# Even mixer: queries' projection first, the convolution's mean ahead of the attention, three sets of head buffers, and reciprocal roots on VectorE

## The chip, the cores and the metric

The kernel runs on one core of one Trainium2 chip. TensorE (PE) multiplies matrices into eight banks of accumulators (PSUM), VectorE (DVE), ScalarE (ACT) and GpSimd (POOL) work on tiles of 128 partitions, and the DMA queues, above all that of SyncE (SP), bring weights from memory. The metric is the device time of one execution in microseconds (us), lower is better; the time given is the median of three runs.

## The reference

Two trunk layers work on 512 latent tokens and 256 context tokens of width 1024. Each layer is a modulated half-step feed-forward block (width 2816), a token mixer, and another such block. Layer 0 has the even mixer, layer 1 the odd one. The change is in the even mixer and in one helper that all norms over the model width use. What the even mixer computes, cut to its core:

```python
def rms_norm(x, g):   # x * rsqrt(mean(x*x) + EPS) * g
def layer_norm(x, g, b):   # (x - mu) * rsqrt(var + EPS) * g + b
def conv_module(u, prm):
    a, g = split(u + glu_b); y = a * sigmoid(g)
    y = depthwise_conv(y, width 31) + dw_b            # 512 channels
    return silu(layer_norm(y, ln_g, ln_b))
def mla_kv(pp, prm, rope):                            # 8 heads
    kvu = rms_norm(pp[..., :256], kv_norm) @ w_ukv    # -> k_nope (64) and v (64) of each head
    k = concat(rms_norm(k_nope), rope(rms_norm(pp[..., 256:288])))
def mla_q(pp, prm, rope):
    q = rms_norm(pp[..., 288:672], q_norm) @ w_uq     # 64 + 32 of each head, both normed, 32 rotated
def even_mixer(hl, hc, prm, ...):
    att = attention(q, k, v)      # latent queries: keys of context and latent; context queries: context keys
    return concat([att, conv_module(pl[..., 672:])]) @ w_out
```

## The kernel before

Products in full fp32 precision are formed as three products of rounded parts: each operand is split into a high part `hi` (a cast, L210) and a low part `lo` (a subtraction, L211), and `hi*hi + lo*hi + hi*lo` is summed in a PSUM bank (L190). PSUM is used as two pairs of banks called `pa`, one pair called `pb`, and two single banks `p`; the helper `pd()` goes round pa, pa, pb. The feed-forward blocks are long rows of such products. A scheduler orders what is not pinned on each engine by its own estimates; instructions passed through `pin` keep their order.

The even mixer before its attention: the input products give the low-rank rows (`natA`, 256 wide, for keys and values; `natB`, 384 wide, for queries). `lora_t` (L869, L871) transposes them on TensorE and splits them. Then come, for each of the six token tiles, the keys' and values' products with `w_ukv` (`up_tile`; ScalarE copies the key part out at L888, the value part at L889 and squares the keys at L891; VectorE sums the squares at L894, takes the root and scales the keys by it, L196); the transposes of `natB`; the rotation of the keys' last 32 columns; and the queries' six tiles with `w_uq`, evacuated at L951, L952 and L954, whose roots, scaling and rotation VectorE does. Head 0's keys and queries are then transposed in four quarters of three tiles each (`quarter`: transposes L923, the high part on ScalarE L926, the low part on VectorE L929).

The attention is a pipeline of 48 items, eight heads of six query tiles, pinned (`flow`). An item has scores (S, L1003), exponentials (L633), a reciprocal of the row sum (L624), a scaling on GpSimd (L625), transposes (L617) and the product with the values (L664); VectorE's row maximum of the scores is L630. Query tiles 0 to 3 see 768 keys, tiles 4 and 5 (context) see 256. In items 1 to 4 of a head the next head's four quarters are formed. The layer norm of the convolution rides in the same pipeline: a list of steps (`conv_ln`), one taken at the end of each item from item `LN0` on. Before, these steps are: the mean over channels in two pieces (L765: ones times the four channel tiles, in one PSUM bank; L770: four subtractions that read the bank), the squares on ScalarE with sums on GpSimd (`sq`, L778), and the reciprocal root, whose steps are `rb_steps`: sums over partitions (L269), `rstd` (L244 to L249: mean plus epsilon on VectorE, Sqrt on ScalarE at L245 with a table load, reciprocal and one Newton step on VectorE), a diagonal matrix (L274), a product that spreads it over partitions (L279) and a copy to the tile `rb` (L282). `rb_steps` stands at nine places of the program, the others in the norms of the feed-forward blocks and mixers.

Another background work is the modulation rows (`mod_dve`): VectorE multiplies rows of the modulation weights by the tile `cb` (128x2048), which holds silu of the conditioning vectors. `cb` is loaded from `in_cB` (L328), put through Silu (L329), and kept.

Of the kernel before, what the change touches and what calls it, by code (L numbers as in the profile page):

```python
# [19 lines left out]
NT = NL + NC  # L20
# [14 lines left out]
LN0 = 8  # L35
# [55 lines left out]
class Kern:  # L91
# [143 lines left out]
    def rstd(self, ss, n, inv_n, mul=None, pin=lambda i: i):  # L235
# [23 lines left out]
    def rb_steps(self, inv_n, nt, pin, buf, t0=0):  # L259
# [11 lines left out]
        def f1():  # L271
            r = self.rstd(c["ps"][:, :k], k, inv_n, None, pin)
# [484 lines left out]
    def conv_ln(self):  # L757
# [4 lines left out]
        def mean(a, b, o):  # L762
            mu = self.p1()[:, 0:b - a]
            for c in range(4):
                pin(nc.tensor.matmul(mu, self.ones, cv[c][:, o:o + b - a], start=c == 0, stop=c == 3))  # L765

            def f():
                for c in range(4):
                    y = cv[c][:, o:o + b - a]
                    pin(nc.vector.scalar_tensor_tensor(y, mu, -1.0 / 512, y, op0=ALU.mult, op1=ALU.add))  # L770
            return f
# [42 lines left out]
    def even_mixer(self):  # L814
# [44 lines left out]

        cq6 = self.rows("B", NT, 6)  # L860
# [21 lines left out]
        Kp = [a.rearrange("p (t h e) -> p t h e", t=2, e=96) for a in Ka]
        for t in range(6):
            i = t % 2
            p = self.pd()
            self.up_tile(p, ckh, ckl, t, wk, 0, 512)
            self.up_tile(p[:, 512:1024], ckh, ckl, t, wk, 512, 512)
            (nc.scalar.copy if EVB[1] else nc.vector.tensor_copy)(K[t][:, :, 0:64], h8(p[:, 0:512]))  # L888
            nc.scalar.copy(V[t], p[:, 512:1024])  # L889
            sq = self.t768()  # L890
            nc.scalar.activation(sq[:, 0:512], p[:, 0:512], AF.Square)  # L891
            if i == 0:
                sK = self.stat(16)
            nc.vector.tensor_reduce(sK[:, i * 8:i * 8 + 8], h8(sq[:, 0:512]), axis=AX.X, op=ALU.add)  # L894
            if i:
                rK = self.rstd(sK, 16, 1.0 / 64)
                kn = Kp[t // 2][:, :, :, 0:64]
                self.tt(kn, kn, rK.rearrange("p (t h) -> p t h", t=2).unsqueeze(3).broadcast_to((128, 2, 8, 64)), ALU.mult, QN_E(nc))
        lora_t(natB, cqh, cql, 3, "qg")
# [719 lines left out]
```

## Time and profile before

| what | value |
|---|---|
| median of three runs | 2865.4 us (2865.26 to 2869.09) |
| profiled execution | 2866.91 us, its span 2865.0 us |
| PE busy | 2792.8 us, 97% of the span |
| DVE busy | 1588.1 us, 55% |
| ACT busy | 858.3 us, 30% |
| POOL busy | 317.0 us, 11% |
| mean granted TensorE clock | 0.99 |
| even mixer, from the keys' and queries' projections to the fourth head | 752.5 to 889.0 us of the span |
| first scores of the attention | 812.53 us |

The busy shares are means over the whole span; the last line names the stretch in which the change works. "Granted clock" is the share of full speed that the chip allowed TensorE in a stretch. A row of a timeline gives start, duration, engine, line, operation, tile written and tiles read, and in square brackets how long the engine had been idle before it and what ended that idle time.

### The profile page before, as it was taken

Reading aid. Unit: us, or ns where it says so; the run is one execution under the profiler, and the core shown is the slowest. Engines: PE = TensorE matmul, PEld = TensorE weight load, DVE = VectorE, ACT = ScalarE, POOL = GpSimd, SP = SyncE. Lnnn points to the kernel's source line nnn. Section 1 sums busy time; section 2 is a strip of 40 time slices with the busy share of each in tenths; the row PEclk is TensorE's granted clock in tenths of the full one; section 3 lists DMA queues with packets and bytes.
Section 4 is the critical chain, followed back from the end, with each engine's and each line's share of the span. In section 5 each row is a group of like instructions: output and inputs, shape, how many; then the busy total and the mean of one; then the engine's idle time right before and its main releaser. Section 6 shows DMA issues by size and latency. Waiting matters only on the chain.

```text
span 2865.0 us, 41335 instructions
## 1 busy us (share of the span) xinstructions
PE 2792.8 (97%) x17180; PEld 2429.3 (85%) x17180; DVE 1588.1 (55%) x2618; ACT 858.3 (30%) x1284; POOL 317.0 (11%) x357
## 2 busy tenths in 40 slices
PE   7999999999978999999999999999999999999999
PEld 5888888887767788888888888888887878898998
DVE  2674675678565576747535432333347689644443
ACT  3221212242456422122122221221224267322222
POOL 1000000030022320000002100000021156300000
PEclk9999999999989999999999999999999999999999
DMA  6343343442200224426411121212133200322232
GB/s 234 126 149 109 116 156 104 133 138 75 72 30 20 63 95 130 151 89 208 160 66 60 60 67 59 66 54 69 61 101 114 60 12 31 96 92 93 90 102 89
DMA packets 80042, 272.22 MB, mean 95 GB/s; under 512 B 9456, under 2 KB 11248, under 8 KB 79728
## 3 DMA queue, kind: packets, MB, share of 16 engines
q1 hardware_dynamic: 72048, 252.11, 27.4%
q10 hardware_dynamic: 6144, 12.23, 1.4%
q0 software_dynamic: 1664, 5.24, 0.5%
q8 instruction: 136, 2.23, 0.3%
q14 instruction: 50, 0.41, 0.0%
HBM read 258.10 MB, written 7.34 MB: 93 GB/s over the span
## 4 chain that ended last, share of the span: by engine, by line
PE 64%; DVE 2%; ACT 1%; DMA 1%; issue 1%; POOL 0%; ACTq 0%; DVEq 0%; POOLq 0%
PE pa L190 39%; PE pb L190 19%; PE p L664 2%; PE pb L617 2%; DMA m<-in_modt 1%; PE pa L1229 1%; PE pa L1003 1%; ACT t L619 0%; DVE sm L630 0%; DVE m L339 0%; PE p L279 0%; PE pa L1255 0%; DVE wl L211 0%; PE p L1217 0%; ACT t L803 0%
## 5 line engine op out<-in xcount | busy, mean ns | idle before, releaser
L210 ACT CAST wh<-r 128x1024 fp32r<-128x1024 f32 (+3 forms) x334 | 341.7, 1023 | 1494.1 <-PE pa L190 778.4
L190 PE MATMUL pa<-B,wh 128*128 128x258 f32 (+2 forms) x1952 | 481.4, 328 | 2.7 <-ACT B L386 2.7
L190 PE MATMUL pa<-C,wh 128*128 128x258 f32 (+2 forms) x1952 | 481.7, 328 | 0.3 <-DVE C L387 0.3
L190 PE MATMUL pa<-B,wl 128*128 128x258 f32 (+2 forms) x1952 | 478.3, 326 | 0.0
L211 DVE TENSOR_TENSOR wl<-r,wh 128x1024 fp32r<-128x1024 f32 (+3 forms) x334 | 400.5, 1199 | 43.6 <-ACT wh L210 37.2
L190 PEld LDWEIGHTS pa<-B,wh 128*128 128x128 f32 x1952 | 303.6, 190 | 37.5 <-ACT B L386 2.7
L190 PEld LDWEIGHTS pa<-C,wh 128*128 128x128 f32 x1952 | 303.4, 190 | 35.0 <-issue 0.7
L190 PEld LDWEIGHTS pa<-B,wl 128*128 128x128 f32 x1952 | 303.6, 190 | 34.6
L190 PE MATMUL pa<-E,wh 128*128 128x512 f32 (+1 forms) x937 | 258.9, 345 | 1.8 <-POOL E L215 1.2
L190 PE MATMUL pb<-B,wh 128*128 128x512 f32 (+1 forms) x992 | 244.3, 327 | 0.0
L190 PE MATMUL pb<-C,wh 128*128 128x512 f32 (+1 forms) x992 | 243.4, 327 | 0.0
L190 PE MATMUL pb<-B,wl 128*128 128x512 f32 (+1 forms) x992 | 242.7, 326 | 0.0
L475 DVE COPY sm<-pa 128x2 f32<-128x2 f32 x115 | 18.2, 158 | 403.2 <-PE pa L190 403.2
L190 PE MATMUL pa<-D,wh 128*128 128x512 f32 (+1 forms) x800 | 207.0, 337 | 0.7 <-ACT D L227 0.6
L190 PE MATMUL pa<-D,wl 128*128 128x256 f32 (+1 forms) x752 | 200.1, 339 | 0.0
L339 DVE SCALAR_TENSOR_TENSOR m<-m,cb 128x1024 f32<-128x1024 f32 x128 | 157.1, 1230 | 28.9 <-DMA m<-in_modt 28.3
L190 PEld LDWEIGHTS pa<-E,wh 128*128 128x128 f32 x937 | 150.2, 188 | 24.8 <-POOL E L215 1.6
L190 PEld LDWEIGHTS pb<-B,wl 128*128 128x128 f32 x992 | 153.9, 190 | 17.9 <-issue 0.5
L190 PEld LDWEIGHTS pb<-B,wh 128*128 128x128 f32 x992 | 153.7, 189 | 17.8 <-issue 1.5
L190 PEld LDWEIGHTS pb<-C,wh 128*128 128x128 f32 x992 | 153.4, 189 | 17.1 <-issue 0.2
L190 PEld LDWEIGHTS pa<-D,wh 128*128 128x128 f32 x800 | 125.4, 188 | 19.9 <-ACT D L227 0.9
L199 DVE SCALAR_TENSOR_TENSOR A<-pa,hg,A 128x256 f32<-128x256 f32 (+1 forms) x96 | 55.3, 613 | 144.8 <-PE pa L190 144.8
(328 smaller groups left out, 4197.7 us busy)
## 6 DMA issues: line engine op xcount, KB each, us to landing
m<-in_modt SPq DMA_DIRECT2D x128, 512.0 KB, 4.2
r<-in_win0a SPq DMA_DIRECT2D x44, 512.0 KB, 3.5
r<-in_win0b SPq DMA_DIRECT2D x44, 512.0 KB, 3.5
r<-in_win1a SPq DMA_DIRECT2D x44, 512.0 KB, 3.4
r<-in_win1b SPq DMA_DIRECT2D x44, 512.0 KB, 3.4
r<-in_wodd SPq DMA_DIRECT2D x18, 512.0 KB, 3.8
r<-in_wout0a SPq DMA_DIRECT2D x20, 448.0 KB, 3.9
r<-in_wout1a SPq DMA_DIRECT2D x20, 448.0 KB, 3.3
```

The costliest lines, as they stand in the source:

```text
L190: self.nc.tensor.matmul(out, l.bitcast(F32R), r.bitcast(F32R), start=st, stop=sp)
L199: self.nc.vector.scalar_tensor_tensor(o, a, s, b, op0=op0, op1=op1)
L210: pin(self.nc.scalar.copy(hi, r))
L211: pin(self.nc.vector.tensor_tensor(lo, r, hi.bitcast(F32), op=ALU.subtract))
L339: nc.vector.scalar_tensor_tensor(o, u, 1.0, self.cb[:, v * 1024:(v + 1) * 1024], op0=ALU.mult, op1=ALU.mult, accum_out=self.mod[L][:, f, v ...
L475: nc.vector.tensor_copy(w2[:, o:o + 2], p[:, so:so + 2])
L617: pin(nc.tensor.transpose(pt[:, ks], P[:, ks], self.col("ident")))
L664: self.pin(self.nc.tensor.matmul(self.po[i * 64:(i + 1) * 64, col:col + 128], v, self.PTs[i][:, kt * 128:(kt + 1) * 128], start=(kt == 0), ...
L1003: self.pin(nc.tensor.matmul(s[:, o:o + b - a], q[:, ts].bitcast(F32R), k[:, a:b].bitcast(F32R), start=j == 0, stop=j == 2))
L1229: self.pin(nc.tensor.matmul(s[:, a:b], q.bitcast(F32R), k[:, a:b].bitcast(F32R), start=j == 0, stop=j == 1))
```

## The change

1. Both `lora_t` stand together, and the queries' products come before the keys' and values'.
2. The weights `w_ukv` are split earlier, before the transposes. Their parts go to the two halves of the tile `cb`, to the area `E3` and to a tile of the `m` pool; therefore `cb` is loaded and put through Silu once more afterwards.
3. The convolution's mean is formed ahead of the attention: eight matmuls into one `pa` pair, one copy by ScalarE with the factor -1/512 into `rb`. In the pipeline four steps `centre` add `rb` to the channel tiles on VectorE, from SBUF alone.
4. Head 0's quarters all come after the keys, queries first, in three rotating pairs (`pd()`).
5. The three sets of head buffers are B0/B1, B3/C3 and E2/E3 in this order.
6. `LN0` goes from 8 to 4, and empty steps (`no`) stand between the squares and between the root's steps.
7. In `rb_steps`, at all nine places, the reciprocal root is taken on VectorE: the value's bits, taken as an integer, are shifted right by one and subtracted from 0x5f3759df, and three Newton steps follow. ScalarE has no Sqrt there any more. The other roots (keys, queries, low-rank rows) keep Sqrt.

```diff
-LN0 = 8
+LN0 = 4
@@ rstd(..., bits=False)
-        pin(nc.scalar.activation(s, v, AF.Sqrt))
-        pin(nc.vector.reciprocal(r, s))
-        pin(nc.vector.scalar_tensor_tensor(t, r, -0.5, v, op0=ALU.mult, op1=ALU.mult))
...
+        if bits:
+            pin(nc.vector.tensor_scalar(s.bitcast(I32), v.bitcast(I32), 1, None, op0=ALU.logical_shift_right))
+            pin(nc.vector.tensor_scalar(r.bitcast(I32), s.bitcast(I32), -1.0, float(0x5f3759df), op0=ALU.mult, op1=ALU.add))
+        else:
+            pin(nc.scalar.activation(s, v, AF.Sqrt))
+            pin(nc.vector.reciprocal(r, s))
+        for _ in range(3 if bits else 1):
+            pin(nc.vector.scalar_tensor_tensor(t, r, -0.5, v, op0=ALU.mult, op1=ALU.mult))
+            pin(nc.vector.tensor_tensor(t, t, r, op=ALU.mult))
+            pin(nc.vector.scalar_tensor_tensor(r, t, 1.5, r, op0=ALU.add, op1=ALU.mult))
@@ conv_ln
+        def centre(c):
+            for a, b, o in LNREG:
+                y = cv[c][:, o:o + b - a]
+                pin(nc.vector.tensor_tensor(y, y, self.rb[:, a:b], op=ALU.add))
-        st = [lambda r=r: mean(*r) for r in LNREG]
-        st += [lambda c=c: sq(c) for c in range(4)]
-        st += [lambda: mm(0), lambda: None, lambda: mm(2), lambda: mm(4)]
+        no = lambda: None
+        st = [lambda c=c: (lambda: centre(c)) for c in range(4)]
+        st += [f for c in range(4) for f in (lambda c=c: sq(c), no)]
+        st += [no, lambda: mm(0), no, no, lambda: mm(2), no, lambda: mm(4), no]
@@ even mixer
+        X = self.cbt()
+        self.cb = None
+        E3 = self.area("E3")
+        wk = []
+        for k, (hi, lo) in enumerate(((X[:, 0:1024], X[:, 1024:2048]), (E3[:, 0:1024], self.mt()))):
+            r = self.raw(self.I["wukv"][k], 1024)
+            self.split(hi, lo, r)
+            wk.append((hi, lo))
...
         lora_t(natA, ckh, ckl, 2, "kvg")
+        lora_t(natB, cqh, cql, 3, "qg")
...  (the loop over the keys' and values' tiles now stands behind that of the queries)
+        bufs = [self.rows(t, NT, 4) for t in (["B0", "B1"], ["B3", "C3"], ["E2", "E3"])]
...
+        mu = self.pd()
+        for a, b, o in LNREG:
+            for c in range(4):
+                nc.tensor.matmul(mu[:, a:b], self.ones, self.cv[c][:, o:o + b - a], start=c == 0, stop=c == 3)
+        nc.scalar.activation(self.rb, mu[:, 0:NT], AF.Copy, scale=-1.0 / 512)
+        for j in (2, 3, 0, 1):
+            quarter(0, j, lambda i: i)
```

The lines of the changed kernel are shifted: 7 more in most of the program (L190 is L191, L244 is L246, L274 is L281, L624 is L631), and L923, L926, L929, L1003 are now L972, L975, L978, L1019.

On TensorE, directly ahead of the attention, the rows before are the last products of a query tile (B parts of the low-rank queries against weights), then half of head 0's transposes, here the two quarters of the queries (E and C hold queries):

```order
L190 MATMUL pa_6437<-wh_6254,B_710_5989 128x256
L190 MATMUL pa_6437<-wl_6255,B_709_5988 128x256
L923 MATMUL pb_6545<-small,E_764_6225 96x128 x2
L923 MATMUL pb_6545<-small,E_765_6226 96x128
L923 MATMUL pb_6551<-small,E_765_6226 96x128
L923 MATMUL pb_6551<-small,C_766_6227 96x128 x2
L1003 MATMUL pa_6557<-B_762_6223,C_763_6224 128x512
```

and in the changed kernel the last products are those of a key and value tile, and the mean (L986) and all four quarters (queries in E and C, keys in A) stand between them and the first scores:

```order
L191 MATMUL pb_6451<-E_709_6006,C_717_6020 128x512
L191 MATMUL pb_6451<-m_6007,B_716_6019 128x512
L986 MATMUL pa_6548<-D_610_4934,ones 128x512 x2
L986 MATMUL pa_6548<-D_611_4935,ones 128x512 x2
L986 MATMUL pa_6548<-D_610_4934,ones 128x256 x2
L986 MATMUL pa_6548<-D_611_4935,ones 128x256 x2
L972 MATMUL pa_6558<-small,E_732_6094 96x128 x2
L972 MATMUL pa_6558<-small,E_733_6095 96x128
L972 MATMUL pa_6570<-small,A_723_6066 96x128 x2
L972 MATMUL pa_6576<-small,A_725_6068 96x128 x2
L1019 MATMUL pa_6584<-B_806_6542,B_807_6543 128x512
```

The mean has moved out of the pipeline to this place, and two quarters more stand in it.

On ScalarE at the same place, the rows before are the queries' last evacuation (L954 squares, L245 the root), two casts of weights of the output product (L210) and the two high parts of head 0's queries:

```order
L954 ACTIVATE t_6458<-pa_6437 128x768
L926 ACTIVATE C_763_6224<-pb_6545,ones 96x384
L210 CAST wh_8215<-r_8213 128x1024
L245 ACTIVATE st_6463<-st_6462 128x32
L210 CAST wh_8279<-r_8277 128x1024
L926 ACTIVATE C_763_6224<-pb_6551,ones 96x384
L633 ACT_TABLE_LOAD
L633 ACTIVATE t_6566,sm_6567<-pa_6557,sm_6564 128x768
```

and in the changed kernel they are the keys' last evacuation and root, the second Silu of `cb` with its table load, the mean's copy (L987) and four high parts:

```order
L949 COPY A_725_6068<-pb_6451 128x8x64
L950 COPY C_778_6335<-pb_6451 128x512
L952 ACTIVATE t_6466<-pb_6451 128x512
L251 ACTIVATE st_6470<-st_6469 128x16
L336 ACT_TABLE_LOAD
L336 ACTIVATE cb_8698<-cb_8698 128x2048
L987 ACTIVATE rb<-pa_6548 128x768
L975 ACTIVATE B_807_6543<-pa_6558,ones 96x384
L975 ACTIVATE B_806_6542<-pa_6576,gcomb 96x384
L640 ACT_TABLE_LOAD
L640 ACTIVATE t_6593,sm_6594<-pa_6584,sm_6591 128x768
```

The reload of `cb` has come in between the keys' root and the high parts that the first scores read.

On VectorE, the convolution's root in the pipeline before (between a low part of a quarter and the next item's reciprocal):

```order
L929 SCALAR_TENSOR_TENSOR B_762_6223<-p_6960,gcomb,B_762_6223 96x384
L244 TENSOR_SCALAR sm_7001<-p_6965 128x6
L246 RECIPROCAL sm_7003<-sm_7002 128x6
L247 SCALAR_TENSOR_TENSOR sm_7004<-sm_7003,sm_7001 128x6
L248 TENSOR_TENSOR sm_7004<-sm_7004,sm_7003 128x6
L249 SCALAR_TENSOR_TENSOR sm_7003<-sm_7004,sm_7003 128x6
L274 TENSOR_TENSOR m_7011<-small,sm_7003 128x768
L624 RECIPROCAL sm_7023<-sm_6945 128x1
```

and in the changed kernel:

```order
L637 TENSOR_REDUCE sm_7092<-pa_7068 128x1
L246 TENSOR_SCALAR sm_7104<-p_7082 128x6
L248 TENSOR_SCALAR sm_7105<-sm_7104 128x6
L249 TENSOR_SCALAR sm_7106<-sm_7105 128x6
L254 SCALAR_TENSOR_TENSOR sm_7107<-sm_7106,sm_7104 128x6
L255 TENSOR_TENSOR sm_7107<-sm_7107,sm_7106 128x6
L256 SCALAR_TENSOR_TENSOR sm_7106<-sm_7107,sm_7106 128x6
...
L281 TENSOR_TENSOR m_7120<-small,sm_7106 128x768
L631 RECIPROCAL sm_7131<-sm_7054 128x1
```

The Sqrt between the first two rows is gone, and the three Newton rows stand there three times; the root has moved behind the quarters, to the last item of head 2.

## Rows read from the trace of the kernel before

**Rows 1.** Busy time of each engine by stage, then the granted clock.
```profile
core 0: us, PE busy (x) PEld busy (x) DVE busy (x) ACT busy (x) POOL busy (x), PEclk, DMA share, GB/s
752.50:776.80 24.30, 21.23 (x107) 16.83 (x102) 13.44 (x26) 16.15 (x31) 0.00 (x0) 1.00 0.09 27
776.80:801.20 24.40, 22.13 (x116) 18.61 (x116) 19.88 (x61) 10.59 (x22) 0.00 (x0) 0.93 0.07 23
801.20:812.50 11.30, 1.27 (x7) 0.55 (x5) 10.67 (x22) 5.12 (x9) 0.00 (x0) 0.63 0.38 128
812.50:823.90 11.40, 10.98 (x56) 9.14 (x54) 7.18 (x13) 8.94 (x17) 2.71 (x3) 0.77 0.03 12
823.90:844.60 20.70, 18.74 (x136) 14.30 (x135) 11.76 (x28) 11.38 (x24) 4.55 (x6) 1.00 0.00 1
844.60:874.60 30.00, 22.22 (x144) 17.42 (x142) 10.53 (x26) 16.28 (x33) 10.81 (x10) 0.77 0.06 18
874.60:889.00 14.40, 13.93 (x128) 11.91 (x127) 11.56 (x26) 10.61 (x23) 4.03 (x6) 1.00 0.11 38
```

**Rows 2.** Timeline of TensorE, a wait between two stages of products.
```profile
776.82 1.20 PE L190 MATMUL pa<-wh,B 128*128 128x512 f32 x2 [0.97 <-DVE B L199]
```

**Rows 3.** Timelines of ScalarE and VectorE: keys' evacuation and scaling, a quarter's parts.
```profile
773.36 0.58 ACT L888 COPY A<-pb 128x512 f32<-128x512 f32 x1
...
803.53 0.59 ACT L926 ACTIVATE C<-pb,ones 96x384 fp32r<-96x384 f32 x1
...
774.95 0.69 DVE L894 TENSOR_REDUCE st<-t 128x8 f32<-128x512 f32 x1 [0.37 <-ACT t L891]
...
779.13 1.22 DVE L196 TENSOR_TENSOR A<-A,st 128x1024 f32<-128x1024 f32 x1
...
805.29 0.61 DVE L929 SCALAR_TENSOR_TENSOR C<-pb,ones,C 96x384 fp32r<-96x384 f32 x1
```

**Rows 4.** Tile cb: its Silu (ns), and its DMA issue (KB, us to landing).
```profile
L329 ACT ACTIVATE cb<-cb x1: 1901/1901/1901, 72.8 to 72.8; 128x2048 f32<-128x2048 f32 x1
...
cb<-in_cB SPq DMA_DIRECT2D x1, 1024.0 KB, 4.8
```

**Rows 5.** Timeline of TensorE, the convolution's mean.
```profile
829.84 3.70 PE L765 MATMUL p<-D,ones 128*128 128x512 f32 x8
...
838.12 2.00 PE L765 MATMUL p<-D,ones 128*128 128x256 f32 x8 [1.31 <-DVE E L929]
```

**Rows 6.** Timeline of TensorE, the convolution's reciprocal root.
```profile
854.49 1.92 PE L269 MATMUL p<-ones,acc 128*128 128x1 f32 x12 [2.06 <-POOL acc L778]
...
868.81 2.08 PE L279 MATMUL p<-m,ones 128*128 128x512 f32 x2 [3.11 <-DVE C L929]
```

**Rows 7.** Timelines of VectorE and ScalarE, the same root.
```profile
856.44 0.16 DVE L244 TENSOR_SCALAR sm<-p 128x6 f32<-128x6 f32 x1 [1.70 <-PE p L269]
...
859.19 0.90 ACT L633 ACTIVATE t<-pa,sm 128x768 f32<-128x768 f32 x1 [5.09 <-PE p L664]
...
860.20 1.28 ACT L245 ACT_TABLE_LOAD   x1
...
861.80 0.19 DVE L246 RECIPROCAL sm<-sm 128x6 f32<-128x6 f32 x1 [5.20 <-ACT sm L245]
...
862.70 0.96 DVE L274 TENSOR_TENSOR m<-small,sm 128x768 f32<-128x768 f32 x1
```

**Rows 8.** The root between feed-forward block and even mixer, and TensorE's first product behind it.
```profile
604.73 0.16 DVE L244 TENSOR_SCALAR sm<-p 128x4 f32<-128x4 f32 x1 [0.30 <-PE p L269]
...
605.46 1.06 DVE L211 TENSOR_TENSOR wl<-r,wh 128x864 fp32r<-128x864 f32 x1 [0.57 <-ACT wh L210]
...
608.52 0.69 DVE L274 TENSOR_TENSOR t<-small,sm 128x512 f32<-128x512 f32 x1
...
612.74 0.61 PE L190 MATMUL pa<-wh,B 128*128 128x288 f32 x2 [1.99 <-ACT B L548]
```

**Rows 9.** Line L279 on TensorE: its idle time before that line, us and times.
```profile
  DVE C L929: 3.1, 1
```

More of the change, by code (lines that the diff above doesn't have):

```diff
@@ L10 @@
 F32R = mybir.dt.float32r
+I32 = mybir.dt.int32
 AF = mybir.ActivationFunctionType
@@ L232, in split, with rstd @@
         self.tt(lo.bitcast(F32R), src, hi, ALU.subtract)
-    def rstd(self, ss, n, inv_n, mul=None, pin=lambda i: i):
+    def rstd(self, ss, n, inv_n, mul=None, pin=lambda i: i, bits=False):
         nc = self.nc
@@ L271, in f1 @@
         def f1():
-            r = self.rstd(c["ps"][:, :k], k, inv_n, None, pin)
+            r = self.rstd(c["ps"][:, :k], k, inv_n, None, pin, True)
             c["dg"] = buf()[:, :nt]
@@ L760, in conv_ln @@
         cv = self.cv
[L762 to L771, printed above, removed]
+        def centre(c):
+            for a, b, o in LNREG:
+                y = cv[c][:, o:o + b - a]
+                pin(nc.vector.tensor_tensor(y, y, self.rb[:, a:b], op=ALU.add))
         def sq(c):
@@ L878, in even_mixer @@
         K = [hv(a[:, i * 768:(i + 1) * 768]) for a in Ka for i in range(2)]
-        V = self.rows("C", 512, 6, 3)
-        wk = [self.unit(self.I["wukv"][k], 1024) for k in range(2)]
         h8 = lambda a: a.rearrange("p (h e) -> p h e", h=8)
[L882 to L899, printed above, removed]
         self.tt(kr, kr, v2(rA, 1).unsqueeze(2).broadcast_to((128, 6, 32)), ALU.mult)
@@ L971, in even_mixer @@
             self.tt(qn, qn, rv(rQ[:, 0:16], 64), ALU.mult, nc.gpsimd if QNP[u] else None)
+        V = self.rows("C", 512, 6, 3)
+        Kp = [a.rearrange("p (t h e) -> p t h e", t=2, e=96) for a in Ka]
+        for t in range(6):
+            i = t % 2
+            p = self.pd()
+            self.up_tile(p, ckh, ckl, t, wk, 0, 512)
+            self.up_tile(p[:, 512:1024], ckh, ckl, t, wk, 512, 512)
+            (nc.scalar.copy if EVB[1] else nc.vector.tensor_copy)(K[t][:, :, 0:64], h8(p[:, 0:512]))
+            nc.scalar.copy(V[t], p[:, 512:1024])
+            sq = self.t768()
+            nc.scalar.activation(sq[:, 0:512], p[:, 0:512], AF.Square)
+            if i == 0:
+                sK = self.stat(16)
+            nc.vector.tensor_reduce(sK[:, i * 8:i * 8 + 8], h8(sq[:, 0:512]), axis=AX.X, op=ALU.add)
+            if i:
+                rK = self.rstd(sK, 16, 1.0 / 64)
+                kn = Kp[t // 2][:, :, :, 0:64]
+                self.tt(kn, kn, rK.rearrange("p (t h) -> p t h", t=2).unsqueeze(3).broadcast_to((128, 2, 8, 64)), ALU.mult, QN_E(nc))
@@ L972, in even_mixer, with quarter @@
         for c in (0, 2):
             self.conv_taps(c, 0, 31)
+        bufs = [self.rows(t, NT, 4) for t in (["B0", "B1"], ["B3", "C3"], ["E2", "E3"])]
+        def quarter(h, j, pin=self.pin):
+            kth, ktl, qth, qtl = (b[0:96, :] for b in bufs[h % 3])
+            p = (self.p1() if pin == self.pin else self.pd())[0:96, 0:384]
+            nat, hi, lo = (K, kth, ktl) if j < 2 else (Q, qth, qtl)
+            t0 = (j % 2) * 3
+            cs = slice(t0 * 128, t0 * 128 + 384)
+            hi, lo = hi[:, cs], lo[:, cs]
+            for t in range(3):
+                pin(nc.tensor.transpose(p[:, t * 128:(t + 1) * 128], nat[t0 + t][:, h, :], self.col("ident")))
+            g = self.gcomb[0:96, :] if j < 2 else self.ones[0:96, 0:1]
+            if HI_ACT:
+                pin(nc.scalar.activation(hi.bitcast(F32R), p, AF.Copy, scale=g))
+            else:
+                pin(nc.vector.tensor_scalar(hi.bitcast(F32R), p, g, None, op0=ALU.mult))
+            f = lambda: pin(nc.vector.scalar_tensor_tensor(lo.bitcast(F32R), p, g, hi, op0=ALU.mult, op1=ALU.subtract))
+            if pin == self.pin and LO_LATER:
+                return f
+            f()
@@ L1022, in mk @@
             return S, n, V_, ex
-        bufs += [self.rows(t, NT, 4) for t in (["B0", "B1"], ["E2", "E3"])]
-        for j in range(2, 3 if Q3 else 4):
-            quarter(0, j, lambda i: i)
         self.flow([mk(h, t) for h in range(8) for t in range(6)], self.I["wo0"], PRE)
```

23 lines of the change are left out of this document (removed).

## The prediction, made before the changed kernel was run

> **What bounds the kernel now.** I read the page's engine table first: TensorE is busy nearly the whole span and no other engine over some 55%, so only stretches in which TensorE stands or is slowed can give much. The page's forty slices put the one soft place of the middle at the even mixer, and a table of windows [rows 1] cuts it into stages; the reader is to see two columns there, TensorE's busy time against the stage's length, and the granted clock.
>
> - The projections (752.5 to 801.2, two rows) hold 43.4 us of busy TensorE in 48.7, so 5.3 us idle; at a clock of 0.93 the second row also loses 24.4 x 0.07 = 1.7 us.
> - The gap before the first scores lasts 11.3 us, with 1.3 us of work in it.
> - Heads 1 and 2 take 20.7 and 30.0 us, where head 3 takes 14.4 with the same attention work. In head 2 there are 7.8 us of idle and a clock of 0.77: the 22.2 busy us are 22.2 x 0.77 = 17.1 us of work at full speed.
>
> So the excess over three equal heads is 65.1 - 43.2 = 21.9 us, and the layer norm of the convolution rides just there. The timelines show it: the mean's matmuls take 3.7 + 2.0 us of TensorE [rows 5]; the root holds everybody [rows 6, 7]. VectorE's mean-plus-epsilon is done at 856.6, ScalarE is then waiting for an exponential's input until 859.2, loads the Sqrt's table at 860.2, and VectorE gets the root only at 861.8, after 5.2 us of idling; the diagonal is written at 862.7 and TensorE stands before L279 for 3.1 us. VectorE's order is fixed, so all later items' row maxima and low parts queue behind that reciprocal.
>
> **The heads: minus 17.1 (bounds minus 9 to minus 20).** The mean leaves the pipeline. The steps now begin at item 4: four centres in items 4 to 7, squares in items 8 to 14, the root in item 17 (the end of head 2), its spreading products in items 20 and 22 (head 3), the scaling in head 4. What is left in heads 1 to 3 beyond 3 x 14.4 = 43.2 is the partition sums and the spreading products, together 17.1 - 14.4 = 2.7 us, which is the work of head 2 above that of head 3 [rows 1]. I add 2.0 us of idle, as much as head 1 has now [rows 1], a stage in which the clock nevertheless stands at 1.00. That makes 47.9 against 65.1: -17.1 after rounding.
> The root itself becomes twelve small operations on VectorE (mean-plus-epsilon, shift, subtraction, nine Newton operations). From the reciprocal's start to the diagonal's, four such operations took 862.70 - 861.80 = 0.90 us, so 0.22 each [rows 7]: 12 x 0.22 = 2.7, with the diagonal 0.96 it is 3.6 us of VectorE in one piece, against 6.3 from 856.44 to 862.70 before. The next item's reciprocal and row maximum queue behind it and the exponential behind them; the score stage runs two items ahead of the transposes, some 5 us at 14.4/6 = 2.4 an item, which is what hides most of it. If that cover is gone it costs up to 3.6, and this is what the 2.0 us of idle is meant for. Four centres cost VectorE 8 operations where 8 subtractions from the bank stood, no longer waiting for TensorE.
> Bounds: if only the mean's 6.3 us (head 1 down to 14.4) and the root's shortening of 2.7 come, -9; if no idle is left in the three heads, about -20.
>
> **The projections: minus 3.2 (minus 0.5 to minus 4.5).** The queries' transposes no longer wait behind the keys' last evacuation, and the keys' weights are there early: the wait of 0.97 [rows 2] goes, and I take it that of the 5.3 us idle 2.4 go in all, a little under half, since this row is the longest kind among them. The transposes of two key quarters (six at 0.15, from the windows' busy time about 0.8 us) move behind the projections. So the last product ends near 801.2 - 2.4 - 0.8 = 798.0; call it T. The clock loss of 1.7 stays. At worst a wait of the keys' products replaces those saved.
>
> **The gap: from T plus 11.3 to T plus 10.5.** Two chains meet at head 0's high parts on ScalarE.
> The keys' own: three evacuations end at T + 1.6 (773.36 to 774.95 [rows 3]); sum of squares 0.69, T + 2.3; from the reduction's start at 774.95 to the scaling's at 779.13 lie 4.2 us with other work between, and without that work five small VectorE operations and the Sqrt, about 1.6; scaling 1.22, so T + 5.2.
> The reload of cb: its last reader is the third product before T's end, so the transfer starts near T - 0.7 and lands 4.8 later [rows 4], T + 4.1. On ScalarE, behind it in program order, stand a table load (1.28 [rows 7]), Silu of 1.90 [rows 4], so T + 7.3; then the mean's copy, 0.8, T + 8.1; then four high parts of 0.59 [rows 3], overlapping a little, T + 10.0; then the last low part, 0.61 [rows 3], T + 10.6. The second chain is the later one. It is a wait that the change adds: queued behind the Silu are the copy, the four high parts and the first exponential. The mean (5.7 us) and the twelve transposes lie within this gap beside it, and cost nothing as long as the reload lasts; without the reload the first scores would come at T + 7.8 (transposes 0.8, two high parts and a low part behind the keys' scaling). First scores thus near 808.5, against 812.5: -4.0 for projections and gap together, bounds -0.7 (projections as before) to -6.7 (no wait on the reload).
> Of the table loads, a row shows 1.28 us, beginning 0.01 after ScalarE's previous work, and the Sqrt 0.01 behind it [rows 7]. The Trainium skill, "ScalarE: Activation LUTs" (What ACT_TABLE_LOAD costs), puts a switch at about 2.66 us, 1283 ns of load and some 1380 of draining. By the row no drain shows; by the rule the reload's extra switch would hold the first scores 1.4 us longer, and the sum would be 1.4 us smaller.
>
> **The other roots: plus 3 (0 to plus 7).** Before the mixers the feed-forward block's last norm is short of cover: TensorE's first product stands 1.99 us at 612.74 [rows 8], behind L244 at 604.73, the diagonal at 608.52, the spreading and the modulation. That chain took 3.8 us with one weight split of 1.06 in it. Now it has twelve small operations, 2.7 us, and the order puts two splits between, 2.1, and an accumulation of about 0.5: 5.3, so +1.5 there, and the same in the second layer, +3. Nothing if the second split is not due yet; at most the whole 12 operations and one more split at both places, about 7. At the other six places the spreading products never kept TensorE waiting (its one idle of 3.1 before L279 is that of head 2 [rows 9]), since feed-forward products are there to run.
>
> **Sum.** -17.1 - 4.0 + 3 = -18.1. The profiled execution took 2866.9, so 2848.8; it lies 1.5 over the median of the runs, so against that: 2847.
>
> **Rivals.**
> 1. Half of it comes back. The root's 3.6 us burst on VectorE falls at the short items that end head 2, where items are shortest; the squares still run on ScalarE and GpSimd, and the 2.06 us wait for GpSimd's sum [rows 6] stands. If head 2 or 3 keeps the 7.8 us of idle that head 2 has today [rows 1]: 2847 + 8 = 2855.
> 2. More comes than summed: the other roots cost nothing (-3), the reload is hidden (-2.7), no idle in the three heads (-2): 2839.
> 3. Slower, through the clock. Stages with waits in them ran at 0.77 and the gap at 0.63 [rows 1]. If the short waits, newly spread over projections, gap and heads, leave the clock at half speed for longer, the 84 us of work from 752.5 to the end of head 2 would run at a mean of, say, 0.70, halfway between these two: 84 x 0.43 = 36, less the 4 us that the sum still holds, +32: 2879. It decides against the change from a mean of about 0.79 in that stretch. Against it: the stage with 2 us of idle in 20.7 ran at 1.00, and the change takes waits away from the heads.
> 4. The reordering does nothing for the front, because the reload pushes the first scores back as far as the projections gain, and the roots cost their 7: 2847 + 4 + 4 = 2855, which joins the first rival.
> The Trainium skill, "SBUF — State Buffer", lists a rule that bears on the centres: a VectorE operation with two SBUF inputs and a GpSimd operation that reads SBUF exclude each other for their whole length. The centres now read two tiles in SBUF. By the rule at most GpSimd's 4.55 us of head 1 [rows 1] would be pushed back; no row of before shows centres of this kind, and the sum without that rule is as given.
>
> **How the numbers follow.** Forecast 0.56 (its own range 2841 to 2852), first and fourth rival 0.24 (2852 to 2859), second 0.12 (2835 to 2841), third 0.08. A measurement of this kernel can tell about 0.2% from no change, 5.7 us, so faster means below 2859.7. Of the first rival's 0.24 some 0.04 goes beyond that bound, of the third's 0.08 some 0.03 ends within 0.2% and 0.05 above. Faster 0.87, same 0.07, slower 0.06. The range is 2837 to 2859.
>
> **What would show it.** Right: the first scores near 808; heads 1 to 3 in 47 to 50 us with the clock at 1.00; no Sqrt load in the pipeline; the mean's matmuls inside the gap; TensorE's first product behind the feed-forward norm one to two us later relative to the last partition sum. Wrong: a wait before L276 or L286 of more than 3 us (first rival), Silu of cb done before the keys' scaling (the reload is hidden), a clock under 0.8 in the windows of heads 1 to 3 (third rival), or later stages, the feed-forward block behind the mixer above all, longer than before, for which nothing is in the sum.

## The result, and the profile after

The changed kernel takes 2847.3 us (median of four runs, 2845.6 to 2850.1) against 2865.3: 0.9935 of the time, 95% interval 0.9923 to 0.9948. The forecast was 2847. The profiled execution spans 2843.7 us, 21.3 less than that of before; 2.4 of these lie ahead of the first mixer, in work that the change hardly touches, and are scatter: two later executions whose programs are alike up to there (e0 and e3 below) reached the same partition sums at 600.0 and 604.5 us. That leaves 18.9.

The table of windows, in the columns of [rows 1], cut at the same events (projections in two pieces, gap, heads 0 to 3):

```profile
753.30:776.80 23.50, 22.44 (x132) 18.86 (x132) 15.78 (x37) 13.25 (x26) 0.00 (x0) 1.00 0.00 1
776.80:794.90 18.10, 18.08 (x82) 14.40 (x81) 17.40 (x40) 13.51 (x27) 0.00 (x0) 1.00 0.26 89
794.90:804.60 9.70, 6.93 (x29) 3.96 (x27) 6.68 (x15) 7.68 (x12) 0.00 (x0) 1.00 0.31 108
804.60:815.70 11.10, 10.43 (x55) 8.41 (x55) 7.17 (x13) 8.47 (x16) 2.73 (x3) 0.85 0.00 0
815.70:829.60 13.90, 13.51 (x119) 11.46 (x119) 11.29 (x28) 11.89 (x26) 6.27 (x6) 1.00 0.01 1
829.60:846.80 17.20, 15.47 (x141) 13.03 (x139) 8.48 (x19) 13.16 (x28) 10.99 (x11) 1.00 0.10 32
846.80:866.40 19.60, 15.95 (x132) 12.41 (x132) 11.20 (x31) 10.25 (x23) 4.57 (x6) 1.00 0.08 24
```

Two things differ from [rows 1]: the projections take 41.6 us where they took 48.5, with 1.1 us of idle left, and the clock is 1.00 in every stage but head 0. Heads 1 to 3 take 50.7 us for 65.1, of which TensorE idles 5.8 us.

In the gap, the timeline of ScalarE shows the reload of cb just where the order put it:

```profile
798.11 0.22 ACT L251 ACTIVATE st<-st 128x16 f32<-128x16 f32 x1 [1.56 <-DVE st L246]
798.35 1.28 ACT L336 ACT_TABLE_LOAD   x1
799.64 1.91 ACT L336 ACTIVATE cb<-cb 128x2048 f32<-128x2048 f32 x1
801.46 0.79 ACT L987 ACTIVATE rb<-pa 128x768 f32<-128x768 f32 x1
802.15 0.57 ACT L975 ACTIVATE B<-pa,ones 96x384 fp32r<-96x384 f32 x1
```

and that of TensorE what waits for it, the transposes of the keys, whose bank holds the mean until ScalarE has copied it; the first scores then wait for the last high part:

```profile
794.77 5.32 PE L986 MATMUL pa<-D,ones 128*128 128x512 f32 x16
...
802.30 0.54 PE L972 MATMUL pa<-small,A 128*96 128x128 f32 x3 [1.55 <-ACT rb L987]
803.42 0.54 PE L972 MATMUL pa<-small,A 128*96 128x128 f32 x3 [0.58 <-DVE B L978]
804.62 0.77 PE L1019 MATMUL pa<-B,B 96*128 96x512 f32 x2 [0.67 <-ACT B L975]
```

The convolution's root on VectorE, which answers to [rows 7], is now one row of twelve small operations at a pitch of 0.2 us, from 847.00 to the diagonal at 849.63, 2.6 us where it took 6.3:

```profile
847.00 0.16 DVE L246 TENSOR_SCALAR sm<-p 128x6 f32<-128x6 f32 x1 [1.47 <-PE p L276]
847.27 0.17 DVE L248 TENSOR_SCALAR sm<-sm 128x6 int32<-128x6 int32 x1
847.48 0.17 DVE L249 TENSOR_SCALAR sm<-sm 128x6 int32<-128x6 int32 x1
...
849.36 0.17 DVE L256 SCALAR_TENSOR_TENSOR sm<-sm,sm 128x6 f32<-128x6 f32 x1
849.63 0.96 DVE L281 TENSOR_TENSOR m<-small,sm 128x768 f32<-128x768 f32 x1
850.51 0.16 DVE L631 RECIPROCAL sm<-sm 128x1 f32<-128x1 f32 x1
850.58 0.94 DVE L637 TENSOR_REDUCE sm<-pa 128x1 f32<-128x768 f32 x1
```

The longest waits of TensorE in heads 2 and 3 are two for GpSimd's scaling in head 2, one of 1.07 us at 852.68 in head 3, shown under e1, and one before the second spreading product:

```profile
831.65 0.88 PE L624 MATMUL pb<-small,t 128*128 128x128 f32 x6 [0.78 <-POOL t L632]
...
841.86 0.88 PE L624 MATMUL pb<-small,t 128*128 128x128 f32 x6 [0.73 <-POOL t L632]
...
863.28 0.70 PE L286 MATMUL p<-m,ones 128*128 128x256 f32 x2 [1.51 <-DVE C L978]
```

Before the first mixer TensorE waits longer than in [rows 8], and once more behind the first projection, where nothing was expected:

```profile
611.71 0.85 PE L191 MATMUL pa<-wh,B 128*128 128x288 f32 x2 [2.30 <-ACT B L555]
...
637.24 0.61 PE L191 MATMUL pa<-B,wh 128*128 128x512 f32 x2 [1.45 <-ACT t L839]
```

### The profile page after: what moved, and what is told of

Same layout as the page of the kernel before. It is cut to its first block, busy times and chain, and to the rows that moved or that the text cites. A ratio compares the mean times of both kernels' runs of the same rounds, so it can differ in the third digit from the quotient of the medians.

```text
span 2843.7 us, 41395 instructions
## 1 busy us (share of the span) xinstructions
PE 2782.6 (98%) x17180; PEld 2419.8 (85%) x17180; DVE 1595.7 (56%) x2681; ACT 848.7 (30%) x1269; POOL 317.2 (11%) x357
## 4 chain that ended last, share of the span: by engine, by line
PE 64%; DVE 2%; ACT 1%; issue 1%; DMA 0%; POOL 0%; ACTq 0%; DVEq 0%; POOLq 0%
PE pa L191 40%; PE pb L191 20%; PE p L671 2%; PE pb L624 1%; PE pa L1242 1%; PE pa L1019 0%; DMA m<-in_modt 0%; ACT t L626 0%; DVE sm L637 0%; DVE wl L212 0%; PE pa L1268 0%; PE p L286 0%; PE p L1230 0%; DVE m L346 0%; ACT t L805 0%
## 5 line engine op out<-in xcount | busy, mean ns | idle before, releaser
L191 PE MATMUL pa<-B,wh 128*128 128x512 f32 (+1 forms) x1984 | 487.8, 327 | 3.2 <-ACT B L393 1.7
L191 PE MATMUL pa<-C,wh 128*128 128x512 f32 (+1 forms) x1984 | 489.2, 328 | 0.3 <-DVE C L394 0.3
L191 PE MATMUL pa<-B,wl 128*128 128x512 f32 (+1 forms) x1984 | 485.7, 326 | 0.0
L191 PEld LDWEIGHTS pa<-B,wh 128*128 128x128 f32 x1984 | 308.3, 190 | 38.3 <-ACT B L393 1.8
L191 PEld LDWEIGHTS pa<-B,wl 128*128 128x128 f32 x1984 | 308.3, 190 | 35.4 <-issue 0.5
L191 PEld LDWEIGHTS pa<-C,wh 128*128 128x128 f32 x1984 | 307.9, 190 | 35.4 <-issue 0.7
L191 PE MATMUL pa<-E,wh 128*128 128x512 f32 (+1 forms) x905 | 252.1, 346 | 0.5 <-DVE E L197 0.5
L191 PE MATMUL pb<-B,wh 128*128 128x512 f32 (+1 forms) x960 | 236.4, 327 | 0.0
L191 PE MATMUL pb<-C,wh 128*128 128x512 f32 (+1 forms) x960 | 236.0, 327 | 0.0
L191 PE MATMUL pb<-B,wl 128*128 128x512 f32 (+1 forms) x960 | 235.6, 326 | 0.0
L191 PE MATMUL pa<-D,wh 128*128 128x512 f32 (+1 forms) x768 | 199.8, 338 | 0.0
L191 PE MATMUL pa<-D,wl 128*128 128x256 f32 (+1 forms) x728 | 194.4, 340 | 0.0
L191 PEld LDWEIGHTS pa<-E,wh 128*128 128x128 f32 x905 | 145.2, 188 | 22.7 <-DVE E L197 0.8
L191 PEld LDWEIGHTS pb<-B,wl 128*128 128x128 f32 x960 | 148.9, 190 | 17.3 <-issue 0.2
L191 PEld LDWEIGHTS pb<-B,wh 128*128 128x128 f32 x960 | 148.7, 189 | 17.3 <-issue 1.5
L191 PEld LDWEIGHTS pb<-C,wh 128*128 128x128 f32 x960 | 148.5, 189 | 16.6
L191 PEld LDWEIGHTS pa<-D,wh 128*128 128x128 f32 x768 | 120.5, 188 | 17.8
```

Of the source, the lines that this page charges most:

```text
L191: self.nc.tensor.matmul(out, l.bitcast(F32R), r.bitcast(F32R), start=st, stop=sp)
```

## The experiments

All are compared by stages, read from the timelines of TensorE of one profiled execution each. The stages are: A, from the partition sums of the feed-forward block's last norm to the first product of the even mixer; B, from there to the first transpose of the low-rank rows; the projections; the gap; the pipeline, from the first scores to the first product with the output weights; C, as A in the second layer. The ratio is that of the medians, with its interval, to the kernel before run on the same chips.

| kernel | A | B | projections | gap | pipeline | C | ratio (95%) |
|---|---|---|---|---|---|---|---|
| before | 9.0 | 140.0 | 48.5 | 11.3 | 138.7 | 9.2 | 1 |
| changed | 10.3 | 141.6 | 41.6 | 9.7 | 124.1 | 10.9 | 0.9935 (0.9923 to 0.9948) |
| e0, changed again | 10.4 | 141.6 | 41.9 | 9.5 | 124.2 | 10.7 | 0.9936 (0.9924 to 0.9949) |
| e1, Sqrt everywhere | 9.0 | 138.3 | 41.9 | 9.7 | 125.2 | 9.2 | 0.9934 (0.9921 to 0.9946) |
| e2, VectorE's root in the convolution only | 9.0 | 138.2 | 42.1 | 9.6 | 125.3 | 9.2 | 0.9928 (0.9916 to 0.9941) |
| e3, no reload of cb | 10.3 | 141.6 | 41.7 | 8.4 | 125.4 | 10.7 | 0.9936 (0.9923 to 0.9950) |
| e4, before with VectorE's roots | 10.4 | 141.5 | 48.5 | 11.2 | 135.6 | 10.9 | 1.0005 (0.9996 to 1.0014) |
| e5, no empty steps | 10.2 | 142.2 | 41.7 | 9.6 | 122.3 | 10.9 | 0.9941 (0.9929 to 0.9954) |
| e6, mean in the pipeline | 10.3 | 141.8 | 41.8 | 7.7 | 130.3 | 10.7 | 0.9966 (0.9954 to 0.9979) |
| e7, keys first | 10.4 | 141.7 | 45.0 | 11.3 | 126.3 | 11.0 | 0.9967 (0.9956 to 0.9979) |
| e8, three edits at once | 9.0 | 139.9 | 41.6 | 8.4 | 122.1 | 9.2 | 0.9905 (0.9891 to 0.9920) |
| e9, e8 with Sqrt everywhere | 9.0 | 139.9 | 41.6 | 8.4 | 125.7 | 9.2 | 0.9912 (0.9896 to 0.9929) |
| e10, keys first, weights late | 10.4 | 141.8 | 42.7 | 12.1 | 124.2 | 10.8 | 0.9953 (0.9938 to 0.9968) |

Where the programs are alike, stages repeat within some 0.5 us, but for the pipeline and B, where a short wait is at times followed by half clock and at times not. The pipeline of e3 is 1.3 us longer than that of the changed kernel with the same instructions: behind the spreading product at the end of head 3's layer-norm work the granted clock is 0.75 in the one and 1.00 in the other (the windows of e3, then of the changed kernel):

```profile
862.60:869.43 6.83, 5.25 (x38) 4.33 (x39) 1.83 (x7) 2.24 (x7) 1.82 (x2) 0.75 0.23 77
```
```profile
861.20:866.41 5.21, 3.66 (x38) 2.90 (x39) 1.37 (x5) 2.21 (x7) 1.81 (x2) 1.00 0.27 87
```

So 1.6 us in a pipeline is not yet a difference between two kernels. Head 3 is 19.6 us in the changed kernel, e0 and e10, but 21.2 in e2, e3, e6 and e7, with the same root; and the last head, with the same instructions everywhere, is 16.3 us at a clock of 1.00 in e5, e8 and e10 and 17.8 to 17.9 in the others (0.90 in the changed kernel and in e9).

**e0** is the yardstick. Expected: 

> The changed kernel once more, as the yardstick of this set. Every theory expects about 2847 us, 0.9935 of the kernel before; a scatter of single executions by some 2 us.

Measured 2845.7 us; its stages are those of the changed kernel within 0.3.

**e1, Sqrt everywhere.**
```diff
-            r = self.rstd(c["ps"][:, :k], k, inv_n, None, pin, True)
+            r = self.rstd(c["ps"][:, :k], k, inv_n, None, pin, False)
```
Expected: 

> The changed kernel with ScalarE's Sqrt back in all nine roots. My theory (the root on VectorE costs about 1.5 us at each of two places before the mixers and saves some 3 to 4 us in the pipeline, where the root's chain is 2.6 us instead of 6.3): 2848 us, TensorE's first product behind the feed-forward norm 1.5 us earlier at both places, heads 2 and 3 some 4 us longer. Rival (the Sqrt and its two table loads were what stalled head 2 altogether): heads 2 and 3 longer by the 7.8 us of idle that head 2 had before, 2853 us.

Measured 2845.4 us. A and C are 1.3 and 1.7 shorter, as my theory has it. Head 2 is unchanged and head 3 is 21.6 us, 2.0 longer than in the changed kernel and 0.4 longer than in the runs whose head 3 fell to half clock; not 4, and not the rival's 7.8. The theory was wrong about the chain: in its new place, behind the quarters, ScalarE comes to the Sqrt at once, and from 842.53 on VectorE to the diagonal at 845.21 the chain takes 2.7 us, as long as VectorE's own root. What Sqrt costs here is the table of the exponential, which is loaded again before the next item:

```profile
842.64 1.28 ACT L251 ACT_TABLE_LOAD   x1
...
847.20 1.28 ACT L640 ACT_TABLE_LOAD   x1 [1.99 <-DVE sm L631]
848.49 0.90 ACT L640 ACTIVATE t<-pa,sm 128x768 f32<-128x768 f32 x1
```

By about as much (1.3 us) the wait before the scores is longer, here in e1 and below in the changed kernel:

```profile
849.54 1.84 PE L1019 MATMUL pa<-B,B 96*128 96x512 f32 x6 [2.39 <-ACT t L640]
852.24 1.66 PE L286 MATMUL p<-m,ones 128*128 128x512 f32 x2
```
```profile
852.68 1.32 PE L1019 MATMUL pa<-B,B 96*128 96x512 f32 x6 [1.07 <-ACT t L640]
854.49 1.12 PE L286 MATMUL p<-m,ones 128*128 128x512 f32 x2
```

B is 3.3 shorter, which I had not foreseen: 1.45 is the wait before L191 at 637.24 shown above, which is not there in e1; most of the rest is clock, 0.90 in the 28 us behind A in the changed kernel and 1.00 in e1, but the kernel before, with Sqrt, had 0.88 there, so that this part is not the root's.

**e2, VectorE's root in the convolution only** (an argument `bits=False` of `rb_steps`, true in `conv_ln`).
```diff
-    def rb_steps(self, inv_n, nt, pin, buf, t0=0):
+    def rb_steps(self, inv_n, nt, pin, buf, t0=0, bits=False):
-            r = self.rstd(c["ps"][:, :k], k, inv_n, None, pin, True)
+            r = self.rstd(c["ps"][:, :k], k, inv_n, None, pin, bits)
-        rb = self.rb_steps(1.0 / 512, NT, pin, self.mt)
+        rb = self.rb_steps(1.0 / 512, NT, pin, self.mt, 0, True)
```
Expected: 

> The changed kernel with the root on VectorE only in the convolution's layer norm, Sqrt at the other eight places. My theory: the two places before the mixers get their 3 us back and nothing else moves, 2844 us. Rival (the longer VectorE chain was covered there, and the 1.4 us later products come from splits that are queued differently by chance): 2847 us.

Measured 2843.3, 2.4 below e0, with overlapping intervals; the stages A and C decide: 1.4 and 1.5 shorter. For these two places the theory held and the rival fell. That nothing else moves did not hold: B is 3.4 shorter, as in e1, and head 3 is 1.6 longer by the half clock told above.

**e3, no reload of cb.** The conv taps are issued ahead of it, which frees D0 and D1:
```diff
-        X = self.cbt()
-        self.cb = None
+        X0, X1 = self.area("D0"), self.area("D1")
-... ((X[:, 0:1024], X[:, 1024:2048]), (E3[:, 0:1024], self.mt()))
+... ((X0[:, 0:1024], X1[:, 0:1024]), (E3[:, 0:1024], self.mt()))
```
Expected: 

> The changed kernel with the first half of the keys' weights split into D0 and D1 in place of cb, so that cb keeps its content and is neither loaded nor put through Silu again. My theory (the table load and Silu, 3.2 us on ScalarE, hold the mean's copy and with it the bank that the keys' transposes wait for): first scores 2 us earlier behind the last product (7.8 instead of 9.8 us), 2845 us. Rival (the mean's 5.3 us of TensorE and the keys' root bound the gap just as well): gap unchanged, 2847 us.

Measured 2846.7 us, no difference by the interval; the gap is 8.4 for 9.7, so 1.3 of the expected 2, and the pipeline is longer by the half clock in head 3. What holds the gap now is the mean: its matmuls end at 803.19, ScalarE's copy begins at 803.24, and the keys' scaling, done at 803.6, is no earlier. Theory and rival both have a part.

**e4, before with VectorE's roots** (the new `rstd`, used in `rb_steps`).
Expected: 

> The kernel before with the roots on VectorE at all nine places and nothing else. My theory: before the mixers TensorE's first product comes 1.3 to 1.5 us later at each of two places, and a like amount is lost in the projection behind the first; in the pipeline the root's chain goes from 6.3 to some 3.6 us and head 2 from 30 to about 26.5; together 0 to +1 us, 2864 to 2865 us. Rival (the Sqrt with its table loads is what stalls head 2, so that its 7.8 us of idle go): head 2 about 22, 2860 us.

Measured 2865.9, ratio 1.0005: nothing, as expected. A, B and C lose 1.4, 1.5 and 1.7, head 2 gains 3.2 (26.9 for 30.1). Two waits of [rows 6] stay in the timeline of TensorE, for GpSimd's sum and before the spreading product:

```profile
856.28 1.83 PE L275 MATMUL p<-ones,acc 128*128 128x1 f32 x12 [2.05 <-POOL acc L784]
...
867.52 2.07 PE L285 MATMUL p<-m,ones 128*128 128x512 f32 x2 [1.50 <-DVE C L935]
```

The Sqrt with its table loads was thus 3.2 of the 15.7 us by which head 2 exceeded head 3, and not the main part.

**e5, no empty steps.**
```diff
-LN0 = 4
+LN0 = 8
-        st += [f for c in range(4) for f in (lambda c=c: sq(c), no)]
-        st += [no, lambda: mm(0), no, no, lambda: mm(2), no, lambda: mm(4), no]
+        st += [lambda c=c: sq(c) for c in range(4)]
+        st += [lambda: mm(0), no, lambda: mm(2), lambda: mm(4)]
```
Expected: 

> The changed kernel with LN0 at 8 and without the empty steps: four centres in items 8 to 11, squares in 12 to 15, the root in 16, its products in 18 and 19. My theory (what matters is that the mean is gone and the root is short): pipeline 124 to 126 us, 2846 to 2848 us. Rival (the empty steps are what keeps GpSimd's sums ahead of TensorE's partition sums): the wait before the partition sums comes back and what follows it runs at half clock, pipeline 129 us, 2851 us.

Measured 2846.6 us; pipeline 122.3. Part of the rival came all the same. Before the partition sums there is a wait again, by the profile for a low part on VectorE and not for GpSimd's sum, and the clock behind it is 0.50 (845.4 to 848.5):

```profile
845.46 2.69 PE L276 MATMUL p<-ones,acc 128*128 128x1 f32 x12 [1.83 <-DVE B L978]
```

With it head 2 takes 21.8 us for 17.3. Head 3, in which the waits around the spreading products are gone, takes 15.6 for 19.6. Together they are 37.4 us for 36.8 in the changed kernel, so the pipeline is not shorter there: 1.6 us of its gain lie in the last head, where the instructions are the same, the rest in heads 0 and 1. The empty steps move waits from one head into the next; the gain does not come from them.

**e6, mean in the pipeline** (the old `mean` with its two steps and two empty ones in place of the four `centre`, from item 4 on; no matmul ahead of the attention).
Expected: 

> The changed kernel with the mean formed in the pipeline again, as before (two steps of four matmuls, subtraction from the bank), everything else kept. My theory (the mean's 5.3 us lie in the gap beside the keys' root and cost nothing there, and 5.7 us of TensorE in the pipeline): gap 9 to 9.7 us as it is, pipeline 130 us, 2852 us. Rival (the mean and its copy hold the gap): gap 2 us shorter, pipeline 130, 2850 us.

Measured 2853.7 us, 7.9 above e0. The pipeline is 130.3, and head 0, in which the mean now lies, 15.9 for 11.1:

```profile
815.75 3.60 PE L772 MATMUL p<-D,ones 128*128 128x512 f32 x8
820.21 1.89 PE L772 MATMUL p<-D,ones 128*128 128x256 f32 x8
```

The gap is 7.7, not 9.7: here the rival was right, the mean and its copy hold the gap by 2 us. By the stages moving the mean still gains 4.2 us, 6.1 in the pipeline less 1.9 in the gap. Of these, 1.6 is the half clock in head 3 that e2, e3 and e7 have too; 2.6 are the mean's own. The medians are further apart than these stages explain.

**e7, keys first** (the loop over keys and values stands ahead of the queries' again, head 0's quarters in the order 0, 1, 2, 3).
Expected: 

> The changed kernel with the keys' and values' products ahead of the queries' again; the early weights, both transposes together and the early mean are kept. My theory (the queries' longer chain of squares, roots and rotation belongs behind other products, not at the end): projections 42 us as now, gap 12 us instead of 9.7, 2848 to 2849 us. Rival (the order is what removed the projections' waits): projections 46 us, gap 12, 2853 us.

Measured 2855.8 us. Projections 45.0, gap 11.3. Neither theory had the place: the second Silu of cb falls into the queries' stage here, with its table load (ScalarE's rows), and TensorE waits there for banks that ScalarE empties (TensorE's rows). The first of these waits is gone in e10, which has no reload; the second is 1.06 us there, and the kernel before had one of 1.39 in the same stage, so it goes with the keys' place and not with the Silu alone:

```profile
781.28 1.28 ACT L336 ACT_TABLE_LOAD   x1
782.58 1.91 ACT L336 ACTIVATE cb<-cb 128x2048 f32<-128x2048 f32 x1
```
```profile
785.24 0.73 PE L191 MATMUL pa<-wh,B 128*128 128x512 f32 x2 [1.45 <-ACT t L941]
793.45 0.74 PE L191 MATMUL pa<-wh,B 128*128 128x512 f32 x2 [1.66 <-ACT t L941]
```

**e10, keys first, weights late** (e7 with `wk = [self.unit(...)]` ahead of the keys' loop, no use of cb).
Expected: 

> The run with the keys first, and in addition the keys' weights split where they were before, in the ring of weight tiles, with no use of cb. Theory (the early weights are what took the rest of the projections' waits): projections 47.5 us where the run with the keys first had 45.0. Rival (putting all five transposes together did it): 45 us. Of the kernel before, projections took 48.5 us, with 0.8 of the keys' quarters in them.

Measured 2853.2 us (0.9953); projections 42.7. The early weights are not what took the waits; the theory fell. Without the reload only one wait of 1.06 for ScalarE remains in the queries' stage. What e10 still shares with the changed kernel is the five transposes together and head 0's quarters behind the projections, and that is worth 48.5 - 42.7 = 5.8, of which 0.8 is the quarters' own work. No run parts these two. The queries' place ahead of the keys is seen in the gap: 12.1 here against 8.4 in e3, both without a reload, though e3 also splits the weights early.

**e8, three edits at once:** e2, e3 and e5 together.
Expected: 

> The changed kernel with three edits at once: VectorE's root only in the convolution's layer norm, the keys' weights in D0 and D1 (no second load and Silu of cb), and no empty steps (LN0 8). My theory (each edit acts at its own place): stages before the mixers shorter by 1.3, about 1.5 and 1.6, gap 8.4, pipeline 122.5, together 7 us below the changed kernel: 2839 us. Rival (the gains of the single edits are scatter of the clock and not their own): 2843 us or more.

Measured 2839.5 us, 0.9905, 0.003 below the changed kernel's ratio. The two intervals do not touch, so it beats both kernels. A, C, the projections and the gap came as in the single runs. B is 139.9 where e2 had 138.2 (in the 28 us behind A the clock is 0.88 here and 1.00 there), and 1.6 of what the pipeline gains is the last head again.

**e9, e8 with Sqrt everywhere.**
Expected: 

> The same with Sqrt on ScalarE in the convolution's layer norm too, so that no root is on VectorE. My theory (the short chain is worth what the wait before the exponential showed, 2.4 against 1.1 us, and the half clock behind it): pipeline 2 to 4 us longer, 2842 us. Rival (with the mean gone the root has slack either way): 2839 us.

Measured 2842.0 us, pipeline 125.7 for 122.1, 2842 expected. The intervals of e8 and e9 overlap (0.9891 to 0.9920, 0.9896 to 0.9929), and of the 3.6 us in the pipeline 1.6 lie in the last head and 0.7 in head 0, where the two programs are the same. Heads 2 and 3, in which the root stands, are 1.4 longer. One item earlier than in e1, Sqrt's chain is long again, 5.8 us from 844.11 to the diagonal at 849.95, for ScalarE is behind an exponential when the sums are ready:

```profile
844.11 0.16 DVE L246 TENSOR_SCALAR sm<-p 128x6 f32<-128x6 f32 x1 [2.87 <-PE p L276]
849.05 0.19 DVE L252 RECIPROCAL sm<-sm 128x6 f32<-128x6 f32 x1 [4.77 <-ACT sm L251]
```

VectorE's chain takes 2.6 us in e8. So the short root is worth about 1.4 us at this one place, by one profile of each; that the time came out at 2842 is in part the clock.

## Why the prediction was right

The time was met to a microsecond, but partly by luck: the heads gave 2.7 us less than forecast and a stage without a term (B) lost 1.6, while the projections and the gap gave 4.5 more. By steps (18.9 us in the profiles, 18.0 between medians, 18.1 forecast):

- **Heads.** Mechanism right, size too large: heads 1 to 3 gave 14.4 for 17.1 (the whole pipeline 14.6). The clock came back to 1.00 and the mean's work left, but the 2.0 us of idle allowed for heads 1 to 3 were 5.8. In head 2 three waits for GpSimd's scaling, beside the squares, make 1.7 of it. In head 3 the 1.07 before the scores is the burst that was feared: the row maximum stands behind the root and the diagonal until 850.58 and is done at 851.5, and the exponential follows at 851.64 (the profile names transposes that ended at 851.6 beside it). The 1.51 before the second spreading product waits for a quarter's low part. So did the 3.1 before L279 in the kernel before [rows 9], where the diagonal, begun and not written at 862.70, was done five us earlier; with VectorE's root (e4) 1.50 of it stayed, so about half of it was not the root's, as the prediction had it. The form of the root was also the smaller part: with Sqrt at the new place (e1) heads 1 to 3 take 52.8 us, with VectorE's root 50.7 to 52.4. What the new place of the root brings by itself is not shown: it has no run of its own.
- **Projections.** The step that failed most: -6.9 for -3.2, outside its own bounds of -0.5 to -4.5. I took it that 2.4 of 5.3 us idle go, since 0.97 was the longest wait of its kind. It was not: another stood before a late query tile, and behind the wait of [rows 2] the clock was 0.52.

```profile
794.66 0.73 PE L190 MATMUL pa<-wh,B 128*128 128x512 f32 x2 [1.39 <-ACT t L954]
```
```profile
776.80:779.50 2.70, 2.68 (x6) 2.12 (x7) 2.70 (x9) 0.60 (x1) 0.00 (x0) 0.52 0.61 205
```

In the changed kernel 4.2 us of idle went, and the clock loss of 1.7 with them, which I had let stand. In e10, with the transposes together and the quarters behind the projections, 3.2 of the idle and all of the clock loss are gone, the wait of [rows 2] among them; with the queries first and the weights early it is 1.1 us more. Half clock behind a wait is part of its price, as the clock of 0.93 in [rows 1] had shown.
- **Gap.** From T + 9.7, forecast T + 10.5. The transfer landed 4.8 us behind its issue at 794.27, at T + 4.1 as worked out. But ScalarE's table load had begun at 798.35, before that, so that more than half of its 1.28 us was hidden; and the first scores waited for the last high part, not for the last low part, which the sum had put before them. Wrong was that the mean costs nothing there as long as the reload lasts: e6, which keeps the reload, has a gap of 7.7. Without the reload (e3) the gap is 8.4, for a forecast of 7.8.
- **Other roots.** +1.3 and +1.7 for +1.5 twice, by the chain that was forecast: from L246 to the diagonal 5.2 us, for 5.3 worked out and 3.8 before. e1 and e2 take the loss back. Not foreseen was the wait of 1.45 behind the first projection; B lost 1.6 us.
- **The Trainium skill's price of a table switch**, "ScalarE: Activation LUTs" (What ACT_TABLE_LOAD costs), is not borne out by these rows: the load ran from 798.35 to 799.63, Silu began at 799.64, and no 1.38 us of draining lie on either side.
- **Rivals.** None took place as a whole. Part of the first did: idle stayed in heads 2 and 3. The clock went the other way from the third. The centres did hold up GpSimd, which the prediction priced at 4.55 us at most: 1.9 us of GpSimd came (last section), and head 1 is 13.9 us where e6, without centres, has 13.6.
- **Signs.** The signs of being right came, with heads 1 to 3 just outside, at 50.7 for 47 to 50. Later stages are not longer: from the first product with the output weights to the second layer's partition sums 1196.5 us for 1197.2, and 707.6 for 707.4 behind C.

Two slips of the prediction change nothing: without idle its own terms give -19.2 for the heads, not -20, and its chances add up to 0.88 for faster, not 0.87.

## What to carry to other kernels

Where one engine is busy nearly all the time, look for the stage in which its clock and its busy share fall together; taking away the short waits there gives back the waits and the clock behind them, so price them with both. A chain of small operations on a busy in-order engine is cheap where others have work to do and costs its length where everyone waits for it; decide such a replacement for each place, not for the helper. A chain that crosses to a second engine takes as long as that engine lets it wait: Sqrt's took 6.3, 5.8 and 2.7 us at three places of the pipeline, VectorE's 2.6 us wherever it stood. So try another place as well as another algorithm. When two things fill a gap, removing one shows what stood beside it: here 9.7 us became 8.4 without the reload and 7.7 without the mean; a kernel without both was not run.

## What the runs showed of the hardware that was not expected

- The same instructions ran a stretch at a granted clock of 0.75 in one kernel's execution and at 1.00 in another's, after equal waits (1.51 us before the spreading product in both; e3 and the changed kernel). A single profile can therefore be off by 1.6 us in such a stage.
- A table load on ScalarE began (798.35) while the data of the activation behind it had not landed (799.1); before an exponential in the pipeline of the kernel before (864.66) the load had come only after 1.65 us of idling for the row maximum. In the changed kernel the load before the first exponential went ahead too, at 804.59, three us before the row maximum. When a load goes ahead of its activation's data, these rows do not settle.
- GpSimd's scaling took two and three times as long beside the centres, additions on VectorE that read two tiles in SBUF. In the changed kernel the scaling of 768 columns at 817.00 and that of 256 at 818.75 each span one channel tile's centre, two additions; in e6, without centres, the same two take 0.91 and 0.48 us:

```profile
817.00 1.79 POOL L632 TENSOR_SCALAR t<-t,sm 128x768 f32<-128x768 f32 x1 [2.33 <-DVE sm L631]
...
818.75 1.54 POOL L632 TENSOR_SCALAR t<-t,sm 128x256 f32<-128x256 f32 x1
```
```profile
817.07 1.02 DVE L772 TENSOR_TENSOR D<-D,rb 128x512 f32<-128x512 f32 x2
...
818.93 1.01 DVE L772 TENSOR_TENSOR D<-D,rb 128x512 f32<-128x512 f32 x2
```

Each is longer by 0.9 to 1.1 us, about the 1.0 of the two additions beside it, while the additions themselves are as short as where GpSimd stands (1.01 at 815.74).
